# One timeline-ordered block around the projections, the gated DeltaNet and the products between them

## The chip, the cores and the metric

The kernel runs on one core of one Trainium2 chip. The metric is the device time of one launch in microseconds (us). The engines are named as in the profile: PE is TensorE (matrix products), DVE is VectorE, ACT is ScalarE, POOL is GpSimd, SP is SyncE, which here issues most weight transfers.

## What is computed

Two layers of a backbone block over 768 tokens (256 context tokens, 512 latent tokens) of width 1024. Each layer normalizes and modulates the stream, multiplies it with one wide input projection, and splits the columns among four mixers: a bidirectional gated DeltaNet (GDN), windowed attention, a gated MLP over chunks of tokens, and a bidirectional mLSTM. Their outputs go through one output projection, then an MLP follows. The reference, cut to what matters here:

```python
def token_mixing(hx, hc, w_in, ...):
    zx = split_cols(hx @ w_in)
    zc = split_cols(hc @ w_in)
    a_x, a_c = gdn_mixer(zx[0:6], zc[0:6], ...)
    b_x, b_c = swa_mixer(zx[6:9], zc[6:9], swa_sink)
    c_x = gmlp_mixer(zx[9], zx[10], ...)
    d_x, d_c = mlstm_mixer(zx[11:17], zc[11:17], ...)
...
def gdn_scan(q, k, v, g, beta, state):
    '''S_t = a_t (I - b_t k_t k_t^T) S_{t-1} + b_t k_t v_t^T, o_t = S_t^T q_t.'''
    ...
    a = jnp.where(strict, jnp.einsum('nbhik,nbhjk->nbhij', kbeta, k) * decay, 0.0)
    sol = lax.linalg.triangular_solve(a + jnp.eye(GDN_CHUNK), rhs, left_side=True, lower=True)
    u, w = sol[..., :dv], sol[..., dv:]
    ...
    state, o = lax.scan(step, state, (u, w, attn, q_dec, k_dec, g_last))
```

Chunks have 64 tokens; each triangular system is 64x64. The second layer needs only the latent tokens' output, so there the query-side projections run on 512 columns instead of 768.

## The kernel before

Everything is one program of straight code in `flow_kernel`; the layer loop (L597) runs twice. Helpers record nearly every instruction, so their lines recur: `mm` (L179) for matrix products, `act_` (L182) for ACT, `tt` (L185) and `stt` (L188) for DVE.

**Projections.** `gemm` (L492) multiplies 128 columns of the input projection with all tokens. The product keeps fp32 accuracy by three passes: weights are split into `whi` (a rounding, made on ACT) and `wlo` (the remainder, made on DVE) by `wsplit` (L464), the activations into `hhi` and `hlo`, and hi·hi, lo·hi and hi·lo are summed. Over 768 tokens a `gemm` is 48 matmuls (8 slices of depth, 3 passes, pieces of 256 and 512 columns); over latent tokens alone it is 24. `gemm_tok` (L519) gives its result with tokens on partitions, in products of 256 columns called `mmt`: 144 over all tokens, 96 over latent ones. Weights come by DMA on SP's queue into `wst`.

**One layer, in the order in which the code is written.** The gate columns (`gatesT`, L636) are transposed and a chain of small DVE operations makes softplus values of them (`ysp`, `tb`, `tc`; L643 to L660). Six `gemm`s (L684) feed the GDN's convolution over time: four multiply-adds each, on tiles `kq` and `vf` (770 columns). Small operations on `gtmp` (L724, L726) make the decay terms. Then the GDN runs in six steps s = 0 to 5:

- `gdn_pre(s)` makes the decay matrix `E` and the matrix `N` to be inverted;
- `gdn_inv(s)` (L839) inverts I + N in five iterations, each a chain over two engines: PE `t2`, DVE `T2`, PE `yt`, DVE `Y`, DVE transpose `Z`, and again; PE `nw`, ACT `T2`, PE `nw2` and DVE `Y1` then refine the result. The profile leaves out buffer and name endings, so `T2` and `t2` are `T` and `t` there, and `Y1` is `Y`;
- `gdn_kt(s)` scales keys and queries (`kt`, `kd`);
- `gdn_scan(s)` carries the state `St` through two chunks and adds to the outputs `O`.

The scan of step s needs the scan before it; the inverses need nothing of each other but their buffers. In the code, `gdn_scan(s)` is followed by `gdn_pre(s+2)`, `gdn_inv(s+2)` and `gdn_kt(s+1)`. After the GDN the code lists the attention projections `sk`, `sq` (two), `sv` with their rotations (`rope`), the gated MLP's values (`vt`, a `gemm_tok`, with its gelu on ACT and DVE in `tc`), the mLSTM's `lk` and `lq` (two each), the gated MLP's products `sg`, the preparation of the mLSTM's gates (PE `mb`, `aRp`, `blp`, DVE scans, `La`, `MD`, then PE `Mt`, `Ml`; L1115 to L1198), and last the mLSTM's values `va` (a `gemm_tok`). What comes after is the block `mix`, which begins on PE with `decp` and takes `MD`.

**What sets the order.** Each engine works off its own list of instructions in order. The program's framework sets the order of these lists. For most of the program (the main body) it may mix instructions of different places of the code. A region opened with `tc.block(..., schedule_with_timeline_sim=True)` gets its order from a model of the timeline, and none of its instructions can stand before the block's first or after its last; on every engine a branch marks where it begins or ends. Before the change only the `mix` block of each layer (L1500) is such a region:

```python
        with tc.block(name=f"mix{l}", schedule_with_timeline_sim=True):
            for _ in states():
                pass
```

Of the kernel before, what the change touches and what calls it, by code (L numbers as in the profile page):

```python
# [140 lines left out]
def flow_kernel(ctx, tc, t, out, dbg=None, stop=None):  # L141
# [455 lines left out]
    for l in range(DEPTH):  # L597
# [62 lines left out]
        stt(sp, sp, 2.0, u, MUL, ADD)  # L660


        kq = [gd.tile([128, 2, GAP], F32, name=f"kq{j}") for j in range(2)]
        vf = [gd.tile([128, GAP], F32, name=f"vf{j}") for j in range(2)]
        unit = []
# [540 lines left out]
        if stop == "A":  # L1206
            return


        gzp = pb.enter_context(tc.tile_pool(name="gzp", bufs=1))  # L1210
        sw2 = pb.enter_context(tc.tile_pool(name="sw2", bufs=2))
# [412 lines left out]
```

## Time and profile before

| | us |
|---|---|
| median of 3 runs | 1973.41 (1973.05 to 1975.29) |
| the profiled execution | 1960.3 |
| its span, first to last instruction | 1958.5 |
| PE busy | 1881.4 (96% of the span) |
| DVE busy | 1196.3 (61%) |
| ACT busy | 754.2 (39%) |
| POOL busy | 101.1 (5%) |

The profiled execution is one run on its own and lies 13 us under the median; its rows give durations, and differences found with them are set against the median. The mean granted clock of PE over the span was 0.979 of full speed. A busy PE is not PE at its peak: in the GDN's steps its short matmuls are counted busy nearly throughout.

### The profile page before, as it was taken

What the parts mean: (1) busy time and instruction counts of PE and PEld (TensorE: products, weight loads), DVE (VectorE), ACT (ScalarE), POOL (GpSimd) and SP (SyncE); (2) the same over time, 40 slices, a digit from 0 to 9 for tenths busy, and PEclk for the clock granted to TensorE, in tenths of its full rate; (3) what the DMA queues carried; (4) which work ended last, traced back from release to release, by engine and by line L of the source; (5) the groups of instructions that cost most, each with busy time, mean ns of one, the idle gap of its engine ahead of it and who ended that gap; (6) DMA issues with size and microseconds to landing.
All of it is one profiled execution on the core that took longest, in us unless ns stands there. A gap on an engine that the chain in (4) does not pass through costs nothing.

```text
span 1958.5 us, 33935 instructions
## 1 busy us (share of the span) xinstructions
PE 1881.4 (96%) x14107; PEld 1539.8 (79%) x14107; DVE 1196.3 (61%) x2210; ACT 754.2 (39%) x1528; POOL 101.1 (5%) x163
## 2 busy tenths in 40 slices
PE   6999999999899999999999999999999999999998
PEld 3877778778777888888888878677777778888887
DVE  3878875666659566435535349788777754444443
ACT  4652234455424312312213236534355543333242
POOL 0021210000000000000000000212100000000001
PEclk8999989999799999999999999999999999999999
DMA  9220001111364345335423222201011323333332
GB/s 324 80 52 24 23 13 44 57 55 44 120 203 128 109 140 147 94 116 151 129 84 122 81 62 54 63 23 34 23 44 33 102 76 103 97 97 97 97 97 76
DMA packets 225634, 172.28 MB, mean 88 GB/s; under 512 B 19042, under 2 KB 207816, under 8 KB 225480
## 3 DMA queue, kind: packets, MB, share of 16 engines
q1 hardware_dynamic: 219104, 153.38, 26.5%
q10 hardware_dynamic: 4680, 10.70, 1.5%
q0 software_dynamic: 1696, 6.03, 0.9%
q8 instruction: 110, 1.80, 0.4%
q14 instruction: 44, 0.36, 0.1%
HBM read 162.75 MB, written 7.34 MB: 87 GB/s over the span
## 4 chain that ended last, share of the span: by engine, by line
PE 82%; DVE 10%; ACT 4%; DMA 3%; issue 1%; POOL 0%; DVEq 0%; ACTq 0%; SPq 0%; POOLq 0%
PE mm L179 63%; PE mmt L179 2%; PE num L179 1%; PE ops L179 1%; DVE kq L188 1%; DMA wst<-w_in 1%; PE pv L179 1%; DVE wlo L185 1%; PE yt L179 1%; DVE Y L185 1%; PE adaps L179 1%; PE pT L1340 1%; PE t L179 1%; PE Eps L179 1%; PE yps L179 1%
## 5 line engine op out<-in xcount | busy, mean ns | idle before, releaser
L182 ACT ACTIVATE whi<-wst 128x512 fp32r<-128x512 f32 (+1 forms) x388 | 241.7, 627 | 682.2 <-PE mm L179 623.5
L179 PE MATMUL mm<-hhi,whi 128*128 128x512 f32 (+3 forms) x1344 | 477.8, 361 | 12.8 <-ACT hhi L182 11.4
L179 PE MATMUL mm<-hlo,whi 128*128 128x512 f32 (+3 forms) x1344 | 479.4, 357 | 1.5 <-DVE hlo L188 1.3
L179 PE MATMUL mm<-hhi,wlo 128*128 128x512 f32 (+3 forms) x1344 | 475.3, 356 | 0.1
L185 DVE TENSOR_TENSOR wlo<-wst,whi 128x512 fp32r<-128x512 f32 (+1 forms) x388 | 265.1, 687 | 313.3 <-ACT whi L182 309.4
L179 PEld LDWEIGHTS mm<-hhi,whi 128*128 128x128 f32 (+1 forms) x1344 | 251.9, 188 | 55.4 <-ACT hhi L182 14.9
L179 PEld LDWEIGHTS mm<-hlo,whi 128*128 128x128 f32 (+1 forms) x1344 | 253.1, 188 | 39.9 <-DVE hlo L188 3.6
L179 PEld LDWEIGHTS mm<-hhi,wlo 128*128 128x128 f32 (+1 forms) x1344 | 252.2, 188 | 39.0 <-issue 2.8
L179 PE MATMUL mm<-fhi,whi 128*128 128x512 f32 (+1 forms) x784 | 276.0, 352 | 0.0
L179 PE MATMUL mm<-flo,whi 128*128 128x512 f32 (+1 forms) x784 | 276.0, 352 | 0.0
L179 PE MATMUL mm<-fhi,wlo 128*128 128x512 f32 (+1 forms) x784 | 274.6, 350 | 0.0
L188 DVE SCALAR_TENSOR_TENSOR x<-mm,mod,x 128x256 f32<-128x256 f32 (+1 forms) x122 | 79.7, 653 | 142.4 <-PE mm L179 142.3
L179 PEld LDWEIGHTS mm<-fhi,whi 128*128 128x128 f32 x784 | 148.4, 189 | 21.7 <-ACT whi L182 0.8
L179 PEld LDWEIGHTS mm<-fhi,wlo 128*128 128x128 f32 x784 | 148.1, 189 | 19.7
L179 PEld LDWEIGHTS mm<-flo,whi 128*128 128x128 f32 x784 | 148.4, 189 | 19.2
L188 DVE SCALAR_TENSOR_TENSOR adacc<-adw,scT,adacc 128x1024 f32<-128x1024 f32 x84 | 105.8, 1281 | 28.3 <-DMA adw<-ada_w 28.2
L185 DVE TENSOR_TENSOR flo<-r,fhi 128x768 fp32r<-128x768 f32 (+1 forms) x64 | 52.6, 824 | 39.2 <-ACT fhi L182 39.1
L182 ACT ACTIVATE fhi<-r 128x768 fp32r<-128x768 f32 (+1 forms) x64 | 47.2, 740 | 66.8 <-DVE r L185 66.8
L179 PE MATMUL mm<-mlo,whi 128*128 128x512 f32 (+1 forms) x192 | 71.0, 370 | 1.3 <-DVE mlo L185 1.3
L179 PE MATMUL mm<-mhi,whi 128*128 128x512 f32 (+1 forms) x192 | 70.6, 368 | 0.4 <-ACT mhi L182 0.4
L179 PE MATMUL mm<-mhi,wlo 128*128 128x512 f32 (+1 forms) x192 | 70.0, 365 | 0.0
L182 ACT ACTIVATE r<-mm 128x256 f32<-128x256 f32 (+1 forms) x96 | 49.1, 514 | 31.5 <-PE mm L179 31.5
(404 smaller groups left out, 2712.3 us busy)
## 6 DMA issues: line engine op xcount, KB each, us to landing
wst<-mlp_w SPq DMA_DIRECT2D x128, 512.0 KB, 4.0
adw<-ada_w SPq DMA_DIRECT2D x96, 512.0 KB, 4.3
wst<-w_in SPq DMA_DIRECT2D x44, 512.0 KB, 3.7
wst<-w_out SPq DMA_DIRECT2D x64, 128.0 KB, 3.1
xd<-x ACTq DMA_DIRECT2D x8, 384.0 KB, 3.5
x<-xd POOLq DMA_DIRECT2D x8, 384.0 KB, 5.2
xs<-x ACTq DMA_DIRECT2D x4, 512.0 KB, 6.9
wst<-w_in SPq DMA_DIRECT2D x8, 256.0 KB, 3.4
```

Source lines behind the costliest of these rows:

```text
L179: T.matmul(o, lhsT=l, rhs=r, start=start, stop=stop)
L182: S.activation(out=o, in_=i, func=f, **kw)
L185: (eng or V).tensor_tensor(out=o, in0=a, in1=b, op=op)
L188: V.scalar_tensor_tensor(out=o, in0=a, scalar=s, in1=b, op0=op0, op1=op1)
L1340: T.transpose(o[:, 256 * i + 128 * g:256 * i + 128 * g + 128], Ps[g][:, 128 * (i0 + i):128 * (i0 + i) + 128], ident)
```

## The change

A block of the same kind as `mix` is opened behind the softplus chain and closed behind `va`, in each layer. Nothing else is changed; the instructions are the same but for the branches.

```diff
@@ -660,6 +660,8 @@
         stt(sp, sp, 2.0, u, MUL, ADD)
 
 
+        blk = ctx.enter_context(ExitStack())
+        blk.enter_context(tc.block(name=f"gdn{l}", schedule_with_timeline_sim=True))
         kq = [gd.tile([128, 2, GAP], F32, name=f"kq{j}") for j in range(2)]
         vf = [gd.tile([128, GAP], F32, name=f"vf{j}") for j in range(2)]
         unit = []
@@ -1206,6 +1208,8 @@
         if stop == "A":
             return
 
+        blk.close()
+
 
         gzp = pb.enter_context(tc.tile_pool(name="gzp", bufs=1))
         sw2 = pb.enter_context(tc.tile_pool(name="sw2", bufs=2))
```

What this moves is seen in the order of the instructions, layer 0. A name's number is that of its tile; the change shifts it by one.

**DVE at the start of the region.** Before, the remainders `wlo` of the first convolution weights stand ahead of and among the operations of the softplus chain, and the convolution's `kq` among them:

```order
L185 TENSOR_TENSOR wlo_665<-wst_662,whi_664 128x512
L188 SCALAR_TENSOR_TENSOR hlo_506<-hy_507,mod0_121,hhi_505 128x512
L185 TENSOR_TENSOR wlo_743<-wst_740,whi_742 128x512
L185 TENSOR_TENSOR wlo_669<-wst_662,whi_668 128x512
L185 TENSOR_TENSOR ysp_634<-gatesT_626,tokp0_267 128x192
L185 TENSOR_TENSOR ysp_634<-ysp_634,cst_85 128x192
L648 TENSOR_SCALAR ysp_634<-ysp_634 128x192
L185 TENSOR_TENSOR wlo_747<-wst_740,whi_746 128x512
L185 TENSOR_TENSOR tb_635<-ysp_634 128x192
L188 SCALAR_TENSOR_TENSOR kq0_658<-ta_672,prm0_265,kq0_658 128x770
L651 TENSOR_SCALAR tc_636<-tb_635 128x192
```

Now the chain stands by itself up to the branch, then come twelve operations on `gtmp` (the first and the last are shown), two of the convolution, and only then the first `wlo`:

```order
L188 SCALAR_TENSOR_TENSOR ysp_634<-ysp_634,tb_635 128x192
L1211 UNCONDITIONAL_BRANCH
L185 TENSOR_TENSOR gtmp_1097<-ysp_634,tokp0_267 64x6x4
...
L726 TENSOR_SCALAR gtmp_1097<-ysp_634 64x6x4
L188 SCALAR_TENSOR_TENSOR kq0_659<-ta_673,prm0_265,kq0_659 128x770 x2
L185 TENSOR_TENSOR wlo_666<-wst_663,whi_665 128x512
L185 TENSOR_TENSOR wlo_670<-wst_663,whi_669 128x512
L188 SCALAR_TENSOR_TENSOR kq0_659<-ta_673,prm0_265,kq0_659 128x770
```

On PE the transposes `gatesT` are followed by the branch and four matmuls of the first `gemm` (both pieces of columns, with `whi`), and the next one there takes `wlo_666`: it moved from before the chain to behind it.

**DVE at the end of the last inverse (s = 5).** `T2`, `Y`, `Z`, `Y1` are the inverse's, `kd` and `rr` the scan's; before, the weights' remainders `wlo` and the gated MLP's gelu (`tc`, `vt`) stand between:

```order
L185 TENSOR_TENSOR rr_3529<-Vs_3502,rps_3520 128x256
L185 TENSOR_TENSOR T2_3262<-t2_3253,lvl_394 128x512
L188 SCALAR_TENSOR_TENSOR tc_4093<-tc_4093,vt_3901 128x512
L185 TENSOR_TENSOR wlo_4202<-wst_4199,whi_4201 128x512
L185 TENSOR_TENSOR Y_3281<-Y_3249,yt_3264 128x512
L1052 TENSOR_SCALAR tc_4093<-tc_4093 128x512
L185 TENSOR_TENSOR wlo_4206<-wst_4199,whi_4205 128x512
L185 TENSOR_TENSOR Z_3282<-Z_3250,zt_3284 128x512
L185 TENSOR_TENSOR vt_3901<-vt_3901,tc_4093 128x2x256
L188 SCALAR_TENSOR_TENSOR tc_4101<-tc_4101,vt_3901 128x512
L1052 TENSOR_SCALAR tc_4101<-tc_4101 128x512
L188 SCALAR_TENSOR_TENSOR Y1_3354<-nw2_3337,Y_3281 128x512
```

Now:

```order
L185 TENSOR_TENSOR Y_3250<-Y_3218,yt_3233 128x512
L864 STREAM_TRANSPOSE Z_3251<-Y_3250 128x512
L185 TENSOR_TENSOR kd_3504<-vkT_3513,kds_1125 128x256
L185 TENSOR_TENSOR rr_3530<-Vs_3503,rps_3521 128x256
L185 TENSOR_TENSOR T2_3263<-t2_3254,lvl_394 128x512
L185 TENSOR_TENSOR Y_3282<-Y_3250,yt_3265 128x512
L185 TENSOR_TENSOR Z_3283<-Z_3251,zt_3285 128x512
L188 SCALAR_TENSOR_TENSOR Y1_3355<-nw2_3338,Y_3282 128x512
L1124 TENSOR_SCALAR bm_4426<-mb_4422 128x48
```

What stood between has moved ahead of the third step: on PE the last `mmt` of `va`, which is the last product of any projection of the region, now stands ahead of the last product (`zt`) of the second inverse (s = 1) in layer 0, and in the third iteration of the second inverse in layer 1. Behind it PE has the inverses of s = 2 to 5, the scans and the small products alone.

**PE at the end of the region.** Before, the projections `lk` and `lq` (`mm`) and the products `sg` stand ahead of the gate preparation (`mb`, `aRp`, `blp`, `Mt`, `Ml`), and the 144 `mmt` of `va` around and behind it:

```order
L179 MATMUL mm_4335<-hhi_505,wlo_4331 128x512
L179 MATMUL sg_4386<-wb_633,vt_3901 64x128 x8
L179 MATMUL sg_4396<-wb_633,vt_3901 64x128 x4
L179 MATMUL sg_4402<-wb_633,vt_3901 64x128 x8
L179 MATMUL sg_4412<-wb_633,vt_3901 64x128 x4
L179 MATMUL mb_4421<-ysp_634,cst_85 128x24 x2
L179 MATMUL mb_4421<-ysp_634,ones_87 128x48
L179 MATMUL mmt_4516<-whi_4521,hhi_442 128x256
...
L179 MATMUL mmt_4517<-whi_4521,hlo_443 128x256
L1136 MATMUL aRp_4438<-cst_85,tc_4429 64x128 x4
L179 MATMUL blp_4448<-cst_85,tc_4429 64x2 x6
L179 MATMUL mmt_4517<-wlo_4522,hhi_442 128x256
```

Now the last scan of s = 5 (`yps`, `sps`, `ops`, `rps`) stands there, then the gate preparation and the branches, and then the `mix` block with `decp`:

```order
L179 MATMUL blp_4449<-cst_85,tc_4430 64x2 x6
L179 MATMUL rps_3573<-St_3561,kt_3498 64x64 x8
L179 MATMUL ops_3584<-kt_3498,St_3561 64x64 x8
L179 MATMUL yps_3593<-rr_3582,Y1_3355 64x64 x8
L179 MATMUL ops_3584<-ATb1_1145,yy_3602 64x128 x4
L1138 MATMUL aRp_4439<-cst_85,tc_4430 64x128 x4
L1138 MATMUL aRp_4445<-cst_85,tc_4430 64x128 x2
L179 MATMUL Mt_4497<-cst_85,tc_4466 128x64 x6
L179 MATMUL Ml_4506<-cst_85,mlast_4477 128x64 x6
L1211 UNCONDITIONAL_BRANCH
L1504 UNCONDITIONAL_BRANCH
```

The projections that stood on either side of `aRp`, `Mt` and `Ml` moved in front of the GDN's steps 2 to 5.

## Rows read from the trace of the kernel before

**Rows 1.** Page, part 1: busy time of each engine.

```profile
PE 1881.4 (96%) x14107; PEld 1539.8 (79%) x14107; DVE 1196.3 (61%) x2210; ACT 754.2 (39%) x1528; POOL 101.1 (5%) x163
```

**Rows 2.** Windows, all instructions: window, length, busy PE, PEld, DVE, ACT, POOL; clock; DMA.

```profile
164.10:300.70 136.60, 128.52 (x2125) 101.28 (x2125) 106.68 (x202) 43.88 (x111) 24.14 (x24) 0.96 0.06 17
300.70:355.50 54.80, 53.23 (x477) 47.30 (x476) 28.89 (x68) 19.92 (x44) 4.40 (x7) 1.00 0.15 42
...
188.70:215.60 26.90, 25.26 (x440) 20.55 (x441) 22.19 (x45) 5.53 (x11) 5.38 (x5) 1.00 0.08 22
215.60:242.60 27.00, 24.94 (x434) 19.78 (x434) 21.46 (x39) 8.67 (x25) 5.08 (x5) 1.00 0.08 21
242.60:273.20 30.60, 27.75 (x427) 22.53 (x428) 22.40 (x41) 9.20 (x27) 4.99 (x5) 0.83 0.01 3
```

**Rows 3.** Windows, tile mm alone (PE, PEld, DVE, ACT): two stages of layer 0, one of layer 1.

```profile
65.20:164.10 98.90, 79.16 (x408) 62.37 (x409) 0.00 (x0) 7.93 (x17) 0.98 0.22 58
164.10:300.70 136.60, 23.75 (x93) 14.26 (x93) 0.00 (x0) 1.96 (x4) 0.96 0.06 17
...
1186.00:1272.30 86.30, 67.90 (x312) 50.45 (x313) 0.00 (x0) 6.41 (x13) 1.00 0.25 66
```

**Rows 4.** Windows, tile mmt alone (PE, PEld, ACT): two steps of layer 0.

```profile
188.70:215.60 26.90, 10.89 (x57) 7.85 (x57) 0.00 (x0) 1.00 0.08 22
...
242.60:273.20 30.60, 7.23 (x28) 4.92 (x28) 2.10 (x6) 0.83 0.01 3
```

**Rows 5.** Window in one of these steps, all instructions.

```profile
245.60:252.40 6.80, 6.80 (x79) 5.81 (x78) 3.42 (x7) 0.48 (x2) 0.00 (x0) 0.50 0.00 0
```

**Rows 6.** Timeline of DVE: one undisturbed iteration of an inverse in layer 1.

```profile
1283.54 0.68 DVE L185 TENSOR_TENSOR T<-t,lvl 128x512 f16<-128x512 f32 x1
...
1286.72 0.69 DVE L185 TENSOR_TENSOR T<-t,lvl 128x512 f16<-128x512 f32 x1 [0.50 <-PE t L179]
```

**Rows 7.** Timeline of ACT, projections in a row: start, duration, instruction, [idle before, releaser].

```profile
315.33 0.63 ACT L182 ACTIVATE whi<-wst 128x512 fp32r<-128x512 f32 x1 [1.05 <-PE mm L179]
...
319.51 0.63 ACT L182 ACTIVATE whi<-wst 128x512 fp32r<-128x512 f32 x1 [2.14 <-PE mm L179]
```

**Rows 8.** Timeline of PE at the end of layer 0's region, and of layer 1's.

```profile
355.19 0.28 PE L179 MATMUL mmt<-whi,hlo 128*128 128x256 f32 x1
355.31 0.28 PE L179 MATMUL mmt<-wlo,hhi 128*128 128x256 f32 x1
355.52 0.39 PE L179 MATMUL decp<-MD,sel_r 32*128 32x6 f32 x4
...
1433.17 0.39 PE L179 MATMUL decp<-MD,sel_r 32*128 32x6 f32 x4
```

**Rows 9.** Timeline of DVE at the start of layer 0's region.

```profile
65.22 0.36 DVE L185 TENSOR_TENSOR ysp<-gatesT,tokp 128x192 f32<-128x192 f32 x1 [0.28 <-PE gatesT L636]
...
67.06 1.02 DVE L188 SCALAR_TENSOR_TENSOR kq<-ta,prm,kq 128x770 f32<-128x770 f32 x1
...
74.82 1.92 DVE L188 SCALAR_TENSOR_TENSOR ysp<-ysp,tc 128x192 f32<-128x192 f32 x5
...
80.23 0.68 DVE L185 TENSOR_TENSOR wlo<-wst,whi 128x512 fp32r<-128x512 f32 x1
...
81.77 0.17 DVE L185 TENSOR_TENSOR gtmp<-ysp,tokp 64x24 f32<-64x24 f32 x1
81.86 0.16 DVE L724 TENSOR_SCALAR gtmp<-ysp 64x24 f32<-64x24 f32 x1
```

**Rows 10.** Timelines of ACT, DVE and PE: last refinement, scan and gate preparation, layer 0.

```profile
300.74 0.58 ACT L182 ACTIVATE T<-nw 128x512 f16<-128x512 f32 x1
309.58 0.61 DVE L185 TENSOR_TENSOR O<-O,ops 128x64 f32<-128x64 f32 x4 [1.00 <-PE ops L179]
333.20 0.60 PE L1136 MATMUL aRp<-cst,tc 128*64 128x128 f32 x4
347.11 1.01 DVE L188 SCALAR_TENSOR_TENSOR MD<-rhi,cst,ta 64x768 fp32r<-64x768 f32 x1
```

## The prediction

> **What bounds the kernel now.** I read the busy times of the page first: PE is busy in 96% of the span [rows 1], so anything that lets PE wait shows in the time. Then the windows, cut at what begins and ends the region of layer 0. From the end of `gatesT` (65.2) to `decp` (355.5) [rows 8] PE has hardly a gap, but for two different reasons. In the last 54.8 us it is filled by projections, 53.23 us busy against DVE's 28.89 [rows 2]. In the 136.6 us of steps s = 1 to 5 it works off 2125 matmuls [rows 2], of which 93 are `mm` [rows 3] and 144 `mmt` (the gated MLP's values, one whole `gemm_tok`); the other 1888 are the short ones of the GDN, whose pace a chain between PE and DVE sets: one undisturbed iteration of an inverse takes 1286.72 - 1283.54 = 3.18 us [rows 6], and an inverse has five.
>
> The reader is to see in the steps' windows how little of a step is projection, and how little that matters. Step s = 2 (188.7 to 215.6) has 57 `mmt` and takes 26.9 us. Step s = 4 has 28 `mmt` [rows 4] and takes 30.6 us, with a mean clock of 0.83 [rows 2]. So a step keeps its length of some 27 us when filler is taken out: the chain sets it, and filler rides along. Filler that is done elsewhere shortens nothing here, and PE's idle time in a bare step is lost. That is what the change does. By the order, all projections of the region are issued before or among steps 0 and 1; steps 2 to 5 and the gate preparation stand alone.
>
> **The prices.** Between two halves of a full `gemm` lie 319.51 - 315.33 = 4.18 us [rows 7], so a `gemm` takes 8.36 us on PE. `mmt` follow at 0.12 us [rows 8]: 144 take 17.3 us, 96 take 11.5. Half a `gemm` is 12 matmuls of 256 columns and 12 of 512, so one of 512 takes (4.18 - 12 x 0.12)/12 = 0.228 us and a latent `gemm` 24 x 0.228 = 5.5 us.
>
> **Part 1, the head: +11 us a layer.** PE goes straight from `gatesT` into the first convolution `gemm` before. Now it has four matmuls, then needs a `wlo` that DVE makes behind the whole softplus chain, twelve `gtmp` and two `kq`. The chain has 18 DVE operations; five of them in a row take 1.92 [rows 9], so 18 take 6.9, and with the longer reciprocal and the exponential on ACT I estimate 8. Its bounds are 6.9 and the 16.5 us from 65.22 to 81.77 [rows 9], in which other work stands between. `gtmp` follow at 0.09 (81.77, 81.86): 1.1 us; two `kq` of 1.02 and a `wlo` of 0.68 [rows 9]: 2.7. Sum 11.8, less 0.7 for the four matmuls: 11 us, nothing beside it. Bounds: 10 and, with half of that other work, 14. On ACT nothing is late here, and SP's weights come in the same order.
>
> **Part 2, the filled stretch to the end of the inverse of s = 1.** Layer 0 has 13 `gemm`s (108.7 us) and two `gemm_tok` (34.6): 143.3. What step 0 and the convolution need besides is read from before: 98.9 us hold 408 `mm` [rows 3], which are 8.5 `gemm`s or 71.1 us; 27.8 remain. Step 1 costs PE at most what a step costs before besides its filler, (136.6 - 93/48 x 8.36 - 17.3)/5 = 20.6 us, and at least 378 matmuls of 64 columns at a quarter of an `mmt`'s 0.12: 11.3. I take 16, the middle, since here filler covers part of the waits. Sum 187.1. Layer 1 has 7 full `gemm`s (58.5), 6 latent ones (33.0) and 144 + 96 `mmt` (28.8), with the same 43.8: 164.1.
>
> **Part 3, four bare steps: 28.2 us each.** Below, five iterations of 3.18 give 16 us. Above, a step that sat at the lower clock throughout: the 10.2 us at 0.50 in step 4 (0.17 x 30.6 x 2) cost it some 30.6 - 27.0 = 3.6, or 0.35 us for each; at that rate a step at 1.2 GHz for 60% of its time takes 27.0/(1 - 0.6 x 0.35) = 34. The nearest rows are the steps with least filler: 26.9 (s = 2), 27.0 (s = 3) and 30.6 (s = 4) [rows 2]; their mean is 28.2. DVE loses the `wlo` and gelu operations there, and the scan's order behind the inverse stays. Four steps: 112.8.
>
> **Part 4, the tail: 24.4 us, uncovered.** From the last refinement (300.74) to the last `O` (309.58 + 0.61) go 9.5 us; from `aRp` (333.20) to the end of `MD` (347.11 + 1.01) go 14.9 [rows 10]. Before, `lk`, `lq` and `va` covered the latter, and `decp` waited for nothing. Now `aRp` stands behind the last `ops`, `decp` behind `MD`, and the projections that covered them are spent. The same preparation with a second DVE operation queued ahead here or there gives 22 to 28.
>
> **The sum.** Layer 0: 65.2 + 11 + 187.1 + 112.8 + 24.4 = 400.5 against 355.5: +45.0. Layer 1 starts at 1186.0, the end of its `gatesT`, where its first window begins [rows 3], and ends at 1433.2 [rows 8]: 1186.0 + 11 + 164.1 + 112.8 + 24.4 = 1498.3: +65.1. Together +110 on the profiled execution's 1960.3. The same difference on the median, which lies 13 us higher, gives 1973.4 + 110 = **2083 us**. The `mix` blocks and the MLP keep their order and are costed at nothing.
>
> **A rule against the change.** In step 4, while PE ran the chain with few `mmt` between, the clock fell to 0.50, the level of 1.2 GHz, for 6.8 us [rows 5]. The Trainium skill, "TensorE: Matmul & The Clock Gate", section "HAM oscillation — how this bites in real kernels", says that a matrix engine which waits between bursts is throttled again each time and starts each burst cold. By that rule all bare steps would be like step 4 or worse, and the time 2103 or more. The trace agrees only in part: step 2, with 57 `mmt`, kept the full clock.
>
> **The rivals.**
> 1. *The clock is low for most of the bare steps.* For it: step 4 [rows 2, 5]. Against it: short bursts at half speed fill more of the time, and the clock came back within step 4. With 34 us a step: 8 x 5.8 = 46 more, 2129.
> 2. *The clock holds and the chain runs freer without gemms in PE's list.* If half of step 2's 6.8 us of `mmt` delayed its chain, a bare step takes 23.5: 8 x 4.7 = 38 less, 2045. For it: matmuls of a `gemm` stand in front of short ones that are ready. Against it: the five steps' mean in layer 0 is 136.6/5 = 27.3 us [rows 2], and they have little filler.
> 3. *Faster: the inverses of two steps overlap.* They need nothing of each other, and if PE and DVE ran two chains at once a bare step could fall below 28.2 - 110/8 = 14.4 us, the point from which the change gains. At 13 us a step: 8 x 15.2 = 122 less, 1961. Against it: DVE has 22.19 us of work in step 2 [rows 2], with little of it filler, and the order has only one inverse at a time from s = 2 on.
> 4. *Nothing changes,* 1973: the blocks would have to leave the order as it is, and the order shows otherwise.
>
> **How the numbers follow.** Forecast (26 to 31 us a step) 0.45; rival 1 0.28; rival 2 0.22; rival 3 0.03; rival 4 0.02. A measurement of this kernel tells 0.2% (4 us) from no change. Faster is rival 3 alone, the same is rival 4; the rest, 0.95, is slower. The low end takes rival 2 with a head of 10 and a step 1 of 11.3: 2045 - 2 - 9, some 2034; a little of rival 2 lies below, and I set 2030. The high end is rival 1 with a head of 14: 2129 + 6 = 2135.
>
> **What would show it.** In the changed profile: a gap on PE of about 11 us right behind `gatesT`, ended by a `wlo`; no `mm` and no `mmt` from the refinement of s = 1 on; four periods from `T<-nw` to `T<-nw` of 26 to 31 us, clock under 0.9 there; 24 us from the last of these to `decp`. PE's busy share falls to about 91% (1881.4 of some 2070). I am wrong on the main term if bare periods lie under 24 or over 32, on the filled stretch if the second `T<-nw` of layer 0 comes far from 263 (65.2 + 11 + 187.1), and on the whole if the layers' ends move by less than 30 us each.

## The result: slower by 5%, and the profile after

| | before | after |
|---|---|---|
| median, us | 1973.23 (4 runs, 1972.71 to 1975.29) | 2073.42 (4 runs, 2065.79 to 2078.85) |
| ratio of the times | | 1.0503, 95% interval 1.0463 to 1.0543 |
| span of the profiled execution, us | 1958.5 | 2064.0 |
| mean granted clock of PE | 0.979 | 0.935 |
| from the end of `gatesT` to `decp`, layer 0 | 290.3 | 332.0 |
| the same, layer 1 | 247.2 | 307.6 |

The forecast was 2083 us (2030 to 2135). The two regions grew by 41.7 and 60.4 us, together 102.1; the span grew by 105.5. Behind layer 1's region 4.9 us more go, and ahead of layer 0's 1.3 us less. Of the 4.9, 3.1 lie at the start of the `mix` block, where PE's first product behind `decp` waits for ACT (first before, then after):

```profile
1434.50 1.99 PE L179 MATMUL on<-tb,cst 128*128 128x512 f32 x4 [0.95 <-ACT tb L182]
```

```profile
1538.20 3.57 PE L179 MATMUL on<-tb,cst 128*128 128x512 f32 x4 [3.60 <-ACT tb L182]
```

PE's busy share, first line of the page's part 1 (compare [rows 1]):

```profile
PE 1906.3 (92%) x14107; PEld 1583.7 (77%) x14107; DVE 1207.6 (59%) x2210; ACT 755.2 (37%) x1528; POOL 100.6 (5%) x163
```

**The head.** Timeline of PE at the start of layer 0's region (start, duration, instruction, in brackets the idle time before and what ended it):

```profile
63.38 0.56 PE L636 MATMUL gatesT<-cst,ta 32*128 32x32 f32 x6
69.13 0.58 PE L179 MATMUL mm<-hhi,whi 128*128 128x256 f32 x1 [5.19 <-ACT whi L182]
...
77.16 0.58 PE L179 MATMUL mm<-hhi,wlo 128*128 128x256 f32 x1 [6.38 <-DVE wlo L185]
```

The first gap ends with `whi`, which ACT makes only at 68.46, behind its part of the softplus chain (`tb`); before, two `whi` (63.59 and 65.35) stood ahead of that `tb`:

```profile
66.41 0.36 ACT L182 ACTIVATE tb<-tb 128x192 f32<-128x192 f32 x1 [3.38 <-DVE tb L185]
...
68.46 2.17 ACT L182 ACTIVATE whi<-wst 128x512 fp32r<-128x512 f32 x4
```

The second ends with `wlo` of DVE, whose chain is at its end here (compare [rows 9]):

```profile
72.61 0.36 DVE L188 SCALAR_TENSOR_TENSOR ysp<-ysp,tb 128x192 f32<-128x192 f32 x1
...
74.43 2.08 DVE L188 SCALAR_TENSOR_TENSOR kq<-ta,prm,kq 128x770 f32<-128x770 f32 x2
76.42 1.28 DVE L185 TENSOR_TENSOR wlo<-wst,whi 128x512 fp32r<-128x512 f32 x2
```

PE stands from 63.94 to 77.16 but for four matmuls, and the clock is at its lower level from 66.9 to 80.6 (0.50 in that window): the matmuls that follow one another at 0.12 us in [rows 8] start 0.21 us apart here.

**The steps.** Timeline of ACT, the refinement that ends each inverse, layer 0, and in layer 1 where the first bare step begins and where the last one ends:

```profile
216.20 0.60 ACT L182 ACTIVATE T<-nw 128x512 f16<-128x512 f32 x1 [0.35 <-PE nw L179]
266.32 0.60 ACT L182 ACTIVATE T<-nw 128x512 f16<-128x512 f32 x1 [1.58 <-PE nw L179]
292.50 0.60 ACT L182 ACTIVATE T<-nw 128x512 f16<-128x512 f32 x1 [4.97 <-PE nw L179]
318.77 0.60 ACT L182 ACTIVATE T<-nw 128x512 f16<-128x512 f32 x1 [5.34 <-PE nw L179]
345.42 0.60 ACT L182 ACTIVATE T<-nw 128x512 f16<-128x512 f32 x1 [5.34 <-PE nw L179]
369.43 0.60 ACT L182 ACTIVATE T<-nw 128x512 f16<-128x512 f32 x1 [6.26 <-PE nw L179]
...
1407.45 0.60 ACT L182 ACTIVATE T<-nw 128x512 f16<-128x512 f32 x1 [4.42 <-PE nw L179]
...
1506.68 0.60 ACT L182 ACTIVATE T<-nw 128x512 f16<-128x512 f32 x1 [6.41 <-PE nw L179]
```

Four bare steps take 103.1 us in layer 0 and 99.2 in layer 1: 25.8 and 24.8 each. Windows of single steps, all instructions (columns as in [rows 2]); the third is layer 0's tail, from the last refinement to `decp`:

```profile
216.20:266.30 50.10, 49.30 (x646) 43.58 (x645) 27.02 (x49) 13.67 (x35) 5.01 (x6) 1.00 0.12 34
266.30:292.50 26.20, 19.61 (x384) 15.84 (x384) 20.82 (x45) 5.68 (x13) 4.81 (x6) 0.80 0.01 2
369.40:395.90 26.50, 16.19 (x161) 14.31 (x161) 15.45 (x43) 4.13 (x7) 3.61 (x5) 0.56 0.00 1
1407.50:1433.10 25.60, 18.06 (x336) 15.32 (x336) 18.44 (x33) 4.64 (x10) 4.77 (x6) 0.57 0.01 2
1433.10:1458.40 25.30, 18.77 (x384) 14.92 (x384) 18.39 (x34) 6.83 (x21) 4.78 (x5) 0.82 0.01 3
1458.40:1483.80 25.40, 18.21 (x384) 14.58 (x384) 19.81 (x37) 6.80 (x20) 4.80 (x5) 0.86 0.01 2
```

and the first two of these with the tile `mm` alone:

```profile
216.20:266.30 50.10, 12.87 (x70) 10.64 (x69) 0.00 (x0) 1.93 (x4) 1.00 0.12 34
266.30:292.50 26.20, 0.00 (x0) 0.00 (x0) 0.00 (x0) 0.00 (x0) 0.80 0.01 2
```

Step 1 holds the last 70 `mm` and all of `va`, and is 50 us long at the full clock; from there on no projection is left, PE is busy for 17 to 20 of a step's 23 to 27 us, and the steps' mean clock is 0.57 to 0.86.

**The tail.** Timelines of DVE and PE (compare [rows 10]):

```profile
382.41 0.68 DVE L1139 COPY ta<-aRp 64x512 f32<-64x512 f32 x1 [0.78 <-PE aRp L1138]
...
394.73 1.01 DVE L188 SCALAR_TENSOR_TENSOR MD<-rhi,cst,ta 64x768 fp32r<-64x768 f32 x1
```

```profile
395.89 0.79 PE L179 MATMUL decp<-MD,sel_r 32*128 32x6 f32 x4 [0.39 <-DVE MD L188]
```

PE waits 0.39 us for `MD` now, which ends the chain of the gate preparation on DVE; from the last refinement to `decp` go 26.5 us, and 27.1 in layer 1.

### The profile page after: what moved, and what is told of

The parts are those of the page before. It is cut to its first block, busy times and chain, and to the rows that moved or that the text cites. A ratio compares the mean times of both kernels' runs of the same rounds, so it can differ in the third digit from the quotient of the medians.

```text
span 2064.0 us, 33955 instructions
## 1 busy us (share of the span) xinstructions
PE 1906.3 (92%) x14107; PEld 1583.7 (77%) x14107; DVE 1207.6 (59%) x2210; ACT 755.2 (37%) x1528; POOL 100.6 (5%) x163
## 4 chain that ended last, share of the span: by engine, by line
PE 84%; DVE 8%; ACT 3%; DMA 3%; issue 1%; POOL 0%; ACTq 0%; DVEq 0%; SPq 0%
PE mm L179 64%; PE mmt L179 3%; PE ops L179 1%; PE num L179 1%; PE nw L179 1%; PE pv L179 1%; PE yt L179 1%; PE t L179 1%; PE adaps L179 1%; PE pT L1344 1%; DVE Y L185 1%; PE Eps L179 1%; DMA adw<-ada_w 1%; DMA wst<-w_in 1%; PE yps L179 1%
## 5 line engine op out<-in xcount | busy, mean ns | idle before, releaser
L188 DVE SCALAR_TENSOR_TENSOR adacc<-adw,scT,adacc 128x1024 f32<-128x1024 f32 x84 | 105.7, 1282 | 30.6 <-DMA adw<-ada_w 30.4
L185 DVE TENSOR_TENSOR Y<-Y,yt 128x512 f16<-128x512 f16 x60 | 41.2, 686 | 39.1 <-PE yt L179 39.1
```

Of the source, the lines that this page charges most:

```text
L185: (eng or V).tensor_tensor(out=o, in0=a, in1=b, op=op)
L188: V.scalar_tensor_tensor(out=o, in0=a, scalar=s, in1=b, op0=op0, op1=op1)
```

## The experiments

Theories: the **order theory** (the timeline model spends the projections by step 1, and the chains behind them run uncovered), the **wall theory** (a block costs because nothing may cross its ends) and the **clock theory** (PE's low clock in the bare stretches is the price). Every kernel was timed beside the kernel before; the ratio is estimated from all runs of both and is not exactly the quotient of the medians.

| kernel | median, us | before beside it | ratio, 95% interval |
|---|---|---|---|
| `plain` | 2007.82 | 1967.85 | 1.0192, 1.0166 to 1.0217 |
| `head` | 2051.10 | 1967.85 | 1.0419, 1.0394 to 1.0444 |
| `tail_out` | 2097.22 | 1967.85 | 1.0647, 1.0625 to 1.0668 |
| `pin` | 2099.53 | 1967.85 | 1.0665, 1.0645 to 1.0685 |
| `fine` | 2073.94 | 1972.47 | 1.0526, 1.0492 to 1.0560 |
| `plain_head` | 1989.36 | 1972.47 | 1.0111, 1.0061 to 1.0161 |
| `dummy` | 2081.13 | 1972.47 | 1.0558, 1.0521 to 1.0596 |
| `dummy48` | 2106.13 | 1968.04 | 1.0692, 1.0666 to 1.0718 |
| `dummy_tail` | 2086.53 | 1968.04 | 1.0593, 1.0567 to 1.0619 |
| `fine3` | 2039.39 | 1968.96 | 1.0361, 1.0337 to 1.0386 |
| `mix_other` | 1973.45 | 1968.96 | 1.0027, 1.0006 to 1.0048 |

### Walls without the model: plain and plain_head

```diff
-        blk.enter_context(tc.block(name=f"gdn{l}", schedule_with_timeline_sim=True))
+        blk.enter_context(tc.block(name=f"gdn{l}"))
```

> The same block at the same place, but ordered by the framework's other model, the one that orders the main body; within the block every engine keeps nearly the order of the kernel before, with the branches added. Order theory (the loss is lost cover: the timeline model spends all projections by step 1): only the stall at the head stays, about 13 us a layer, so 1999 us, between 1988 and 2006, and steps 2 to 5 keep their projections. Wall theory (that nothing may cross the block's ends costs the time): as slow as the change, 2060 to 2080.

The block's walls cost 1.9%, and the model's order 3.1% more. PE's list per step is that of before, to within a matmul or two. Layer 1's steps have their lengths of before to 0.1 us, and so has step 2 of layer 0; its steps 3 to 5 took 29.8, 27.8 and 29.8 us instead of 27.0, 30.6 and 27.5, at other mean clocks. Windows of steps 2 to 4 (compare [rows 2]):

```profile
204.00:230.90 26.90, 25.24 (x440) 20.54 (x441) 22.21 (x45) 5.55 (x11) 5.38 (x5) 1.00 0.08 22
230.90:260.70 29.80, 27.75 (x435) 22.20 (x433) 21.66 (x39) 8.66 (x24) 5.08 (x5) 0.89 0.07 19
260.70:288.50 27.80, 24.94 (x427) 20.10 (x428) 20.71 (x37) 9.14 (x27) 5.00 (x5) 0.94 0.01 3
```

The order theory holds in the main, and the walls cost more than I had expected, 40 us instead of 26; the time lies 2 us above the range that was given. The stretches up to the first refinement, with the head in them, took 13.1 and 13.8 us longer. Behind `decp` PE waits for ACT, whose work for the `mix` block could not start ahead of the wall (before, 0.51 us at this place):

```profile
378.13 0.39 PE L179 MATMUL decp<-MD,sel_r 32*128 32x6 f32 x4
382.31 0.90 PE L1394 MATMUL lkT<-cst,lk 128*128 128x128 f32 x3 [3.80 <-ACT dec L182]
```

In layer 0 this brings the first `on` only 0.9 us later behind `decp`, since before PE waited there for a transfer; in layer 1 it brings it 3.4 us later. The last stretch of each region, from the last refinement to `decp`, also grew, from 54.8 to 59.8 us and from 31.6 to 35.2. But that is not shown to be the wall's doing: `mix_other`, below, has no block there, the same matmuls and 59.1 and 35.9 us, also at a lower clock than before (1.00). First `plain` in layer 0, then `mix_other` in both layers:

```profile
318.30:378.10 59.80, 57.72 (x477) 51.76 (x475) 26.41 (x64) 16.49 (x40) 4.50 (x7) 0.91 0.13 38
```

```profile
298.60:357.70 59.10, 57.63 (x477) 51.73 (x475) 29.00 (x68) 19.87 (x44) 4.40 (x7) 0.91 0.13 38
1406.90:1442.80 35.90, 34.38 (x334) 31.95 (x332) 20.83 (x51) 10.18 (x18) 3.66 (x6) 0.86 0.11 30
```

So 31 of the 40 us have a place at the walls (27 in the heads, 4 behind `decp`); where the rest comes from stays open.

`plain_head` opens the same block one operation behind `gatesT`:

```diff
+        tt(y, o[:, 0:192].rearrange("p (s g) -> p s g", g=32), bc(tokp[l][:, 0:32], 1, 6), ADD)
+        blk = ctx.enter_context(ExitStack())
+        blk.enter_context(tc.block(name=f"gdn{l}"))
         u = temp("tb")[:, 0:192].rearrange("p (s g) -> p s g", g=32)
         w = temp("tc")[:, 0:192].rearrange("p (s g) -> p s g", g=32)
-        tt(y, o[:, 0:192].rearrange("p (s g) -> p s g", g=32), bc(tokp[l][:, 0:32], 1, 6), ADD)
...
-        blk = ctx.enter_context(ExitStack())
-        blk.enter_context(tc.block(name=f"gdn{l}"))
```

> The plain block, opened behind the first operation on the gate transposes as in head. If the walls cost by what they keep from mixing, the 13 us at the start of each layer's region go and the 5 us at its end (and some 3 behind it) stay: 2008 less 2 x 11, so 1986, between 1978 and 1994. If a block costs by itself, 2000 or more.

The time is as expected, and where the wall stands matters: by the ratios 16 us of what `plain` lost are back. But the parts are not those that were expected. Half of the head is left: the stretches up to the first refinement are still 6.0 and 7.4 us longer than before, and most of that is PE's wait for the first `whi`, which ACT still makes behind its part of the softplus chain:

```profile
69.13 0.58 PE L179 MATMUL mm<-hhi,whi 128*128 128x256 f32 x1 [5.20 <-ACT whi L182]
```

The longer last stretch (60.0 us in layer 0, 35.2 in layer 1) is what `mix_other` has without a wall.

### The wall at the start, with the model: head

The same edit in the changed kernel (with `schedule_with_timeline_sim=True`).

> The changed kernel with the block opened behind the first operation on the gate transposes, so that the softplus chain is inside and may mix with the first convolution. Order theory: the head's stall (63.94 to 77.16 in the changed kernel, 13 us, and some 1.5 us of half clock behind it) falls to some 4 us, nothing else moves: 2073 less 2 x 10, so 2053, between 2046 and 2060. Wall theory: the walls are still there, one operation earlier, so 2065 or more.

Met: up to the first refinement layer 0 takes 144.0 us instead of 152.3 and layer 1 128.2 instead of 139.6, the bare steps stay at 24 to 27 us. In layer 0 the first product of the region still waits 3.4 us. By the ratios (5.03% to 4.19%) the edit gains 17 us.

### Projections behind the block: tail_out

```diff
+        blk.close()
+
         lk = [z3("lk") for j in range(2)]
...
-        blk.close()
```

> The changed kernel with the block closed ahead of the lk and lq projections: these four, the sg products, the gate preparation and va are in the main body again. Order theory: the gate preparation is covered (some 17 us a layer), step 1 becomes bare too: layer 0 from the gates to decp 314 us instead of 332, layer 1 300 instead of 308, so 2048, between 2035 and 2062. Clock theory (the low clock in bare stretches is what costs): one bare step more and one bare tail less, no gain, 2065 to 2080.

Missed, on the slow side. The stretch from the last refinement to `decp` grew from 26.5 to 75.3 us in layer 0, by 48.8 for the 50.7 us of projections that moved there. The projections cover the gate preparation again, but only behind `aRp`: the scan and the wall come first, and PE's clock stands at 0.50 to 0.55 until 362, twenty microseconds into the stretch. How much of the cover each of these takes back was not tried apart. The stretch up to the end of the inverse of s = 1 shrank by only 31.7 us, since step 1 is bare now (31.3 us). So part of the projections had been covering waits in that stretch too. The bare steps of layer 0 take 27.3 us with a mean clock of 0.69 (the last, which has fewer products, 23.9 at 0.64); this run does not separate the clock's share.

### Projections put back behind the steps: pin, fine, fine3

`pin` holds back on PE the matmuls of `lk`, `lq` and `va`:

```diff
+        def after_nw(s):
+            return tc.issue_after(nwm[s].ins)
...
-                o = gemm([win[:, base + 128 * j:base + 128 * j + 128]], h, sg2)
+                with after_nw(1 + 2 * j + i):
+                    o = gemm([win[:, base + 128 * j:base + 128 * j + 128]], h, sg2)
...
+        with after_nw(5):
+            gemm_tok(l, C_LV, list(range(NP)), h,
```

(`nwm[s]` is the last matmul of `nw` in the inverse of s.)

> The changed kernel, in whose block the matmuls of lk, lq, lk, lq are queued on PE behind the refinements of steps 1 to 4 and those of va behind that of step 5. Order theory: each of steps 2 to 5 takes one gemm and grows by 2 us at most to 27 or 28, the tail takes va and stays at 28, and the filled stretch loses what was moved: layer 0 295 us, layer 1 280, so 2008, between 1995 and 2022. If a gemm in a step lengthened it by its own 8.4 us, nothing would be gained but the tail: 2045. Clock theory: with the gemms the clock stays up, and steps 2 to 5 get shorter than the bare 25 us in spite of the added work.

Missed: no better than `tail_out`. A step with one `gemm` takes 34 to 36 us, its bare length and the whole `gemm` of 8.4:

```profile
268.50:303.20 34.70, 28.93 (x433) 23.10 (x434) 20.23 (x38) 8.94 (x24) 4.82 (x5) 0.84 0.06 17
```

The order of `pin` shows why: `nw`, 22 `mm`, `nw2`, 24 `mm`, `t2`. The model sets the matmuls in lumps of half a `gemm` (some 4 us) into waits of a microsecond, and the chain queues behind them. The changed kernel has such lumps in step 1 (24, 28, 35 matmuls of projections on end); the main body's order of the kernel before has pieces of 1 to 8 in layer 0's steps, but for one of 12.

`fine` deals the same matmuls out:

```diff
+        def take(self):
+            if self.used == self.each and self.i + 1 < len(self.marks):
+                self.i, self.used = self.i + 1, 0
+            self.used += 1
+            return tc.issue_after(self.marks[self.i].ins)
...
+                    with deal.take() if deal else ExitStack():
+                        for pi, (w, a) in enumerate(((whi, ahi), (whi, alo), (wlo, ahi))):
...
+                o = gemm([win[:, base + 128 * j:base + 128 * j + 128]], h, sg2,
+                         deal=Deal([mk[s, n, x] for n in range(1, 6) for x in range(2)], 2))
```

> As pin, but each gemm is dealt out over the ten products t2 and yt of the inverse that it stands in, six matmuls behind each, and va in portions of twelve behind the products of the last scan. Theory of the lumps (in pin a gemm stood in two lumps of 22 and 24 matmuls right behind the refinement, with the chain queued behind them, and so lengthened its step by its own 8.4 us): steps 2 to 5 come down from 34 to some 27.5, the tail from 39 to 29, so 2030, between 2015 and 2048. Theory of the spent PE (a step's PE time is full and a gemm costs its length wherever it stands): no change from pin, 2090 to 2105.

Between the two: by the ratios 27 us gained on `pin`, and 44 us short of 2030. Layer 0's steps with 48 `mm` come down to between 30.1 and 32.4 us; layer 1's four take 28.4 to 34.6. Two of layer 0:

```profile
267.50:297.60 30.10, 26.03 (x432) 20.60 (x432) 20.96 (x38) 8.80 (x24) 4.82 (x5) 0.94 0.07 20
297.60:329.40 31.80, 27.66 (x432) 22.04 (x432) 20.65 (x38) 8.87 (x25) 4.85 (x6) 0.87 0.06 18
```

What was left could lie in the size of the pieces or in the weights' work on ACT and DVE; `dummy48`, below, says the pieces. They were not even: a `gemm` lists its matmuls of 256 columns and those of 512 in turn, so six take 0.7 or 1.4 us (by 0.12 and 0.228 us each), and in PE's list ten of 512 columns (2.3 us) stand on end once in each of layer 0's steps. `fine3` deals by columns, six matmuls of 256 or three of 512 columns (0.7 us either way, not 0.36 or 0.68 as the expectation has it), over the products of steps 1 to 5, and sets `va` behind the last scan and the transposes `aRp`. Against `fine`:

```diff
-        def take(self):
-            if self.used == self.each and self.i + 1 < len(self.marks):
-                self.i, self.used = self.i + 1, 0
-            self.used += 1
-            return tc.issue_after(self.marks[self.i].ins)
+        def take(self, cols):
+            i = min(int(self.used // self.each), len(self.marks) - 1)
+            self.used += cols
+            return tc.issue_after(self.marks[i].ins)
...
+                if not (i or j):
+                    dl = Deal([mk[s, n, x] for s in range(1, 6) for n in range(1, 6) for x in range(2)], 512)
```

> The changed kernel with lk, lq, lk, lq dealt by time over the fifty products t2 and yt of steps 1 to 5, three matmuls (0.36 or 0.68 us) behind each instead of six, and va dealt in pieces of six behind the last scan and for the most part behind the transposes aRp, under the gate preparation on DVE. If a piece of up to 0.7 us fits between two products of the chain and one of 1.05 us does not (dummy against dummy48), steps 1 to 5 take 25 to 28 us and the tail 30: layer 0 some 303 us instead of 332, layer 1 some 286 instead of 308, so 2022, between 2008 and 2042. If real gemms still cost their length through their weights on ACT and DVE, steps stay over 30: 2060 to 2080.

The time is met, near the upper end of its range: 1.4 points less than the change, with the same walls, model and instructions. The parts are less good than expected: steps 2 to 5 take 24.7 to 30.0 us, step 1 31.5 and 29.7, the tail 31.6 and 33. The windows of two steps with 36 and 42 `mm` in PE's list, at the full clock:

```profile
264.60:292.30 27.70, 23.93 (x420) 17.75 (x420) 20.00 (x37) 8.57 (x23) 4.81 (x5) 1.00 0.07 21
292.30:321.30 29.00, 26.61 (x458) 20.37 (x458) 21.10 (x39) 8.26 (x24) 4.97 (x6) 1.00 0.07 21
```

### What a bare step has room for: dummy and dummy48

```diff
+        for s in range(2, 6):
+            o = ps("dummy")
+            for n in range(1, 6):
+                for x in range(2):
+                    with tc.issue_after(mk[s, n, x].ins):
+                        for k in range(3):
+                            mm(o, h[k][0][:, 0:128], h[k][0][:, 256:768])
```

> The changed kernel with 30 matmuls of 512 columns (6.8 us on PE, no result of theirs is used) dealt into each of the eight bare steps, three behind each t2 and yt. Order theory: a step has room for them, it goes from 25.5 us to at most 27 and the clock stays up: 2068 to 2088, for 54 us of added PE work. Clock theory (0.35 us lost for each at 1.2 GHz, of which a bare step has 10 to 13): steps fall to some 22 to 23 us and the whole to 2055 or less. Theory of the spent PE: 54 us more, 2127.

Order theory: 54 us of added work cost some 11 us (the ratio against the change's 1.0503; the two intervals overlap by a little). Layer 0's steps 2 to 5, all instructions:

```profile
268.40:296.60 28.20, 25.02 (x414) 17.96 (x414) 20.27 (x43) 5.67 (x13) 4.81 (x5) 0.94 0.01 2
296.60:322.80 26.20, 23.36 (x386) 16.89 (x390) 17.84 (x31) 6.80 (x21) 4.82 (x6) 0.97 0.01 2
322.80:354.40 31.60, 27.96 (x446) 20.23 (x446) 22.45 (x40) 6.81 (x21) 4.86 (x5) 0.86 0.01 2
354.40:377.90 23.50, 20.68 (x370) 15.13 (x370) 16.29 (x36) 3.49 (x9) 3.53 (x4) 1.00 0.01 2
```

The counts of the second and third window are not what was dealt: the tile `dummy` alone has 30 matmuls in each of them,

```profile
296.60:322.80 26.20, 9.56 (x30) 4.87 (x30) 0.97 0.01 2
322.80:354.40 31.60, 10.24 (x30) 5.21 (x30) 0.86 0.01 2
```

and the first products of a scan (`rps`, `ops`) moved across the refinement that parts the two windows, so these two are read together. 6.8 us of work lengthened step 2 by 2.0 us and step 5 by nothing (23.5 against 24.0), 13.7 us lengthened steps 3 and 4 by 4.9 together. Over both layers the eight steps grew by 12.4 us for 54.6 us of work. The clock came up to 0.85 to 1.00 (by the windows from 104 us at 1.2 GHz in the eight steps to 25), and the time did not fall: what the clock gave back the pieces took. How much that is either way is not separated.

`dummy48` has the pieces of `fine` instead, without their weights:

```diff
+            slots = [mk[s, n, x] for n in range(1, 6) for x in range(2)]
...
+                with tc.issue_after(slots[i // 2].ins):
+                    for k in range(3):
+                        mm((o2 if cn == 512 else o)[:, 0:cn], h[k][0][:, 0:128], h[k][0][:, c0:c0 + cn])
```

> The changed kernel with the very matmuls of fine's gemms (48 or 24 a step, in the same pieces of six behind each t2 and yt) dealt into the bare steps, but without their weights: no transfers, no whi on ACT, no wlo on DVE, no evacuation; no result of theirs is used. If fine's steps of 32 us come from the pieces in PE's list, full steps take 31 to 33 us here too and the whole some 2073 + 40, 2105 to 2120. If they come from what a gemm brings to DVE and ACT, full steps take 27 to 28 and the whole stays at 2080 to 2093.

The pieces: 8.4 us of matmuls in the pieces of `fine` lengthen layer 0's steps 2 to 4 by some 5.5 us each (step 5 by 1.7) although DVE and ACT have nothing more to do. Over both layers 61 us of work lengthen the eight steps by 42; in layer 1 two steps with 5.5 us of it, all in matmuls of 512 columns, grew by some 7 each. Steps 3 and 4 of layer 0:

```profile
298.30:330.50 32.20, 28.72 (x432) 22.59 (x432) 19.31 (x35) 6.82 (x20) 4.82 (x5) 0.87 0.01 2
330.50:362.40 31.90, 28.53 (x432) 22.77 (x432) 19.16 (x35) 6.82 (x20) 4.82 (x5) 0.83 0.01 2
```

### The tail's clock: dummy_tail

```diff
+        for m in (mk["y", 10], mk["o", 10], mk["r", 11], mk["y", 11], mk["o", 11]):
+            with tc.issue_after(m.ins):
+                for k in range(24 if m is mk["o", 11] else 4):
+                    mm(o, h[k % 8][0][:, 0:128], h[k % 8][0][:, 256:768])
```

> The changed kernel with 40 matmuls of 512 columns (9.1 us on PE, no result used) behind the products of the last scan and under the gate preparation, in both layers. If the lower clock there (all of the tail's 27 us in layer 1) lengthens the tail, it comes down towards the 24.4 us that the same operations took before, and the whole to 2066 to 2071. If DVE's chain alone sets it, the tail stays at 27 or grows by a us or two: 2072 to 2079.

Inconclusive: the tail grew to 33.0 us because the model set twenty of the added matmuls ahead of `aRp`, and the clock still stood at its lower level for 16 us of it. What the clock costs the tail stays open.

```profile
386.16 4.83 PE L179 MATMUL dummy<-hhi 128*128 128x512 f32 x20
390.83 0.60 PE L1143 MATMUL aRp<-cst,tc 128*64 128x128 f32 x4
```

### The other model for the mix blocks: mix_other

```diff
-        with tc.block(name=f"mix{l}", schedule_with_timeline_sim=True):
+        with tc.block(name=f"mix{l}"):
```

> The kernel before, with its mix blocks ordered by the model of the main body instead of the timeline model. If the timeline model's order costs time wherever there is filler to place, faster than before: 1940 to 1968. If it costs only where a chain between engines needs the filler spread thin, the same or slower: 1970 to 2010.

Slower by 0.27% (0.06 to 0.48), so the second case: in `mix` the timeline model's order costs nothing against the other. But this kernel gives one more reading. Its step 4 has the list of the kernel before, and so have those of `plain` and `plain_head`; only the clock differs. First `mix_other`, then `plain_head`; `plain`'s (27.8 us at 0.94) is shown above, that of before (30.6 at 0.83) in [rows 2]:

```profile
242.50:268.90 26.40, 23.53 (x428) 18.78 (x428) 20.77 (x38) 9.13 (x28) 5.00 (x5) 1.00 0.01 2
```

```profile
247.30:278.00 30.70, 27.83 (x428) 22.55 (x428) 22.46 (x41) 9.21 (x28) 4.99 (x5) 0.83 0.01 2
```

10.2 us at 1.2 GHz lengthen this step by 4.3, or 0.42 us for each.

## Why the prediction was right, and where it was not

**Sign, cause and size.** Slower by 100 us on the median where 110 were forecast. `plain` and the change have the same walls, and 61 us lie between them: the order spends the projections by step 1. That part is shown. Not shown is how much of the 61 us PE's low clock in the bare stretches makes up: `dummy` raised the clock and added work in one. The head's and the tail's places were as described. That the sum comes so near is partly luck: by the trace parts 1, 2 and 4 were put 15 us too low, part 3 was put 23 us too high.

**Part 1, the head.** 13.2 us less 0.7 for four matmuls, 12.5 instead of 11 in both layers; the clock's lower level from 66.9 to 80.6 was not in the sum. "On ACT nothing is late here" is wrong: the first 5.2 us of the gap end with ACT's `whi`. The sum did not suffer, since `wlo` came later still; `plain_head` did, where this wait is what is left. `head` gained 17 us for both layers. The upper bound of 14 does not come out of its rows: half of the other work, (16.5 - 6.9)/2, gives some 15.

**Part 2, the filled stretch.** The second refinement of layer 0 came at 266.3, 202.4 us behind `gatesT`, for a forecast of 198.1; in layer 1 181.2 for 175.1. Less the head's 1.5 us the stretch itself is right within 3 us in layer 0 and 5 in layer 1. But the sum had a hidden assumption, which `tail_out` and `pin` show wrong: that a projection taken out of this stretch shortens it by its own length. 50.7 us taken out shortened it by 32.

**Part 3, the bare steps: the term that was mis-sized.** 28.2 us were put, 25.8 and 24.8 measured: 23 us too much in eight steps. Part of this is the choice of rows: three steps of layer 0, one of them at a clock of 0.83, stood for all eight, while layer 1's four had taken 25.2 to 27.0 before, at 1.00. Two of them:

```profile
1322.60:1349.60 27.00, 26.36 (x425) 19.22 (x424) 24.51 (x48) 14.74 (x43) 5.72 (x6) 1.00 0.08 22
1376.40:1401.60 25.20, 25.20 (x404) 17.68 (x404) 18.04 (x40) 6.85 (x15) 3.54 (x4) 1.00 0.09 23
```

Against the eight steps as they were before, 216.8 us, the bare ones are 14.5 shorter. There the step that failed is "a step keeps its length of some 27 us when filler is taken out". The filler is not free: 6.8 us of it cost a bare step 1.5 us on the mean (`dummy`), and step 2 of layer 0, bare, took 26.2 us at 0.80 where it had taken 26.9 at 1.00. The other half of that term, the price of the clock, was near: 0.35 put, 0.42 measured in step 4. (0.17 x 30.6 x 2 is 10.4 and not 10.2; shorter windows of the step give 6.8 + 3.4 = 10.2.) Rivals 1 and 2 are both true in part and offset each other: the bare steps ran at a mean clock of 0.57 to 0.86, as in rival 1, and came out shorter all the same, as in rival 2. How long a bare step takes at the full clock no run shows; step 3 and 4 of layer 1 took 25.3 to 27.0 us as their time at the lower clock went from 7 to 13 us in the changed kernel and in `head`, which points to less than 25.

The Trainium skill says in "TensorE: Matmul & The Clock Gate", section "HAM oscillation — how this bites in real kernels", that an engine waiting between bursts is throttled anew. The trace agrees with it here: PE lost its full clock for a time in each of the eight bare steps, after a step 1 with projections at 1.00 in layer 0 and 0.93 in layer 1.

**Part 4, the tail.** 26.5 and 27.1 us for 24.4, with `MD` last, as described. The preparation was right (14.0 us in layer 0 from `aRp` to the end of `MD`, for 14.9); the scan ahead of it was not (12.2 us from the last refinement to the last `O`, for 9.5). The tail's mean clock is 0.56; whether that is the reason no run shows.

**What was left out.** The wall at the block's end. ACT's work for the `mix` block stands behind it, and PE waits for it: in layer 1 the first product behind `decp` comes 3.1 us later than before in the changed kernel and 3.4 in `plain`; in layer 0, where PE waited for a transfer before, 0.5 and 0.9. The `mix` blocks, which were costed at nothing, pay this.

**Rival 3** (overlapping inverses) and **rival 4** (no change) did not happen: PE's counts are one inverse to each period, and the bare steps stay above 22.8 us.

## What to carry to other kernels

Filler is worth what it covers. Ordering independent work as early as possible leaves a chain between two engines with nothing beside it later; count in the order how much of it stands beside each step of the chain, and look at the size of the pieces: here pieces of 0.7 us between two products of the chain cost about a quarter of their length (`dummy`), pieces of 0.7 to 2.3 us two thirds (`dummy48`), lumps of 4 us all of it (`pin`); these are the lengths by which the steps grew, whatever the clock did in them. A block's walls cost what they keep from mixing, here 27 us at the start of two blocks and 4 behind their end in `plain`; so look on every engine at what would have stood on either side.

The Trainium skill advises in "Perfetto Trace Analysis", section "Matmul Optimizations", to run matmuls back to back in batches. The batch did run at the full clock here (1.00 in step 1 of layer 0), but the order that made the batch cost 61 us against `plain`.

## What was not expected of the hardware

The same list of instructions took 26.4, 27.8, 30.6 and 30.7 us in one step of four kernels, with mean granted clocks of 1.00, 0.94, 0.83 and 0.83; the last stretch of layer 0's region took 54.8 us at 1.00 before and 59.1 at 0.91 in `mix_other`. Which executions lose the clock in such a stretch is not settled by what stands in its list.
